# Text order for ScalarE and VectorE in a seven-part output projection, modulation rows two ahead, and a matmul of ones behind each flip

## The chip, the cores and the metric

The kernel runs on one core of one Trainium2 chip. The metric is the device time of one execution in microseconds. The kernel before takes 876.53 us (median of 3 runs, 875.68 to 877.57).

A core has five engines that run side by side: TensorE (PE: matmuls, with PEld for its weight loads), VectorE (DVE), ScalarE (ACT), GpSimd (POOL) and SyncE (SP, which here only issues DMAs). Each works through its own list of instructions in order, and semaphores hold an instruction until what it reads is there.

## The reference

The program is a backbone of two layers over 512 latent tokens and 256 context tokens, width 1024, fp32. Layer 0 mixes tokens by retention in both directions, with 4 heads; layer 1 is a chunked gMLP. Both are modulated by vectors made from a conditioning vector.

```python
for i in range(DEPTH):                                # 2 layers
    shift_x, scale_x, gate_x = jnp.split(silu_c @ ada_w[i] + ada_b[i], 3, axis=-1)
    hx = rmsnorm(x, norm_g[i]) * (1 + scale_x[:, None]) + shift_x[:, None]
    out_x, out_c = ...                                # retention (i = 0), gMLP (i = 1)
    x = x + gate_x[:, None] * out_x
return rmsnorm(x, final_g)

# retention, for each head: scores, decay mask, times v; then
o = o * lax.rsqrt(jnp.mean(o * o, axis=-1, keepdims=True) + NORM_EPS)
out = (o * jax.nn.silu(z)) @ w_out                    # w_out: 2048 x 1024
```

## The kernel before, in words

**Precision.** Every fp32 operand is held as a pair: the high part is a ScalarE cast to a short format, the low part is source minus high part, on VectorE. `split` issues these two. `mm3` makes a product of two pairs from three matmuls. So a weight tile of 128x1024 that TensorE multiplies by (named `hl`) is made from a loaded tile (`raw`) by a ScalarE cast and a VectorE subtraction.

**Seven products in place of eight.** Large products go by a scheme with seven block products (a class `Product`). The weight blocks are the quarters B11, B21, B22 as loaded, and the sums T1 and T2 (two raws added on VectorE), T3 and T4 (in this projection added by a DMA that accumulates, issued by POOL). The other operand is split into quarters too: A11, A12, A22 and the sums S1 to S4. The order of the products is B11, B21, T1, T2, B22, T3, T4, with A11, A12, S1, S2, S4, S3, A22.

**The order of instructions.** TensorE's is the order of the text. For ScalarE and VectorE a scheduler chooses, unless the text pins it: while `act.pinned` and `dve.pinned` are set, the class `Queue` ties each instruction of that engine to the one before it in the text. `aside` runs one step of a side job (a Python generator) with both pinned.

**The weight stream.** The object `Q` loads raws, adds T1 and T2, and splits into four `hl` buffers in rotation. `Q.get()` hands out the next tile and first brings the stream two tiles further (`upto`); `upto` ends by doing the raw sum of the tile after that, ahead of its turn.

**Layer 0's second half.** `attend_two` does heads 0 and 1: for each step of two key blocks `score` (matmuls of q and k, named `qk`, into one of two PSUM buffers tagged `tm`; then `pf` = scores times decay on VectorE, and its pair `ph`, `pl`) and, two steps later, `pv` (matmuls by `v`). After the last step of a half of the queries come the root mean square `ss` and `gt` (the gated output), and a flip: eight transposes of `gt` into PSUM, then `turn`, which builds operands from them. The quarters "11", "21" and "12" lie in the buffers `w3`, `dec` and `g1`. The last flip, (1, 1), gives the operands S1, S2, S4 and A22.

`out_two` is the output projection of heads 0 and 1: 14 runs of 24 matmuls (seven names, each for two column halves q0 and q1), with the last flip inside run n = 1. The finished sums go through `snap` (PSUM copied or added) into `acc` by ScalarE. Side jobs run between: `vs` (v of head 2), `ds` (the decay of head 2: loads into `w3` and `g1`, a ScalarE exponential that needs its table loaded, and `dt` on VectorE) and `qs` (q and k of head 2). Then `attend_one(2)`, `project_out(2)`, `attend_one(3)` and `project_out(3)` do heads 2 and 3 one by one.

**The modulation rows.** `background` forms vectors of layer 1 from 32 rows of 512 KB (`ada_piece`): one row is loaded into a `bg` buffer, and the step after multiplies it by a value and adds it to `ada_a` on VectorE. Its steps are spread through layer 0 by hand. Vector 3 (i = 3) uses the buffers `w2` and `w3`, with one row loaded ahead.

**Ones.** `between_modes` is one 128x128 fp32 matmul of ones by ones. It stands behind some groups of transposes or fp32 matmuls, among them the last flip of head 1.

## Time and profile before

| | before |
|---|---|
| median of 3 runs | 876.53 us (875.68 to 877.57) |
| the profiled execution | 875.56 us, span 873.8 us |
| TensorE busy | 856.6 us (98%) |
| VectorE busy | 709.4 us (81%) |
| ScalarE busy | 479.9 us (55%) |
| GpSimd busy | 84.8 us (10%) |

All times in views of the trace count from the start of the span. Nearly all engine work stands under one line, L54, the helper that records it, so the names of tiles tell what an instruction is: in `hl<-raw,hl` the low part of a weight tile is formed, in `quarter<-pst,quarter` an operand sum, in `oA<-quarter,oA` or `oS<-quarter,oS` its low part. The seven-part projection is the stretch from 380.7 to 425.8 us.

### The profile page before, as it was taken

The page shows a single profiled execution, that of the slowest core. Times are in us where ns is not written, and L with a number is a line of the kernel's source. Part 1 is how long each engine was busy: PE and PEld are TensorE (multiplying, and loading weights), DVE is VectorE, ACT ScalarE, POOL GpSimd, SP SyncE. Part 2 cuts the span into 40 slices and gives each one's busy share as a digit, 9 for nine tenths or more (in the row PEclk, how much of TensorE's full clock was granted, in tenths as well). Part 3 has the DMA queues.
Part 4 walks back from the last instruction along what each step waited for, and adds up shares of the span by engine and source line. Part 5 has one row for each costly group of instructions (what it writes and reads, how often), then busy time and mean ns, then how long its engine had stood idle before and what let it go on. Part 6 is the DMA issues. An engine that isn't in the chain of part 4 may idle for free.

```text
span 873.8 us, 17037 instructions
## 1 busy us (share of the span) xinstructions
PE 856.6 (98%) x6820; PEld 818.0 (94%) x6820; DVE 709.4 (81%) x1003; ACT 479.9 (55%) x757; POOL 84.8 (10%) x127
## 2 busy tenths in 40 slices
PE   8999999999999999999999999999999999999996
PEld 7899999999999999889989899999999899899985
DVE  4799899969968875897677879998888478678895
ACT  5466544464355346657672549744666456255434
POOL 0001211211211010010100002021000000000110
PEclk9999999999999999999999999999999999999998
DMA  9945867868967796258984642657555246146532
GB/s 360 403 122 151 248 193 270 254 201 242 303 188 223 232 337 199 87 151 272 239 288 150 217 105 109 203 148 236 175 146 191 51 146 203 39 145 194 121 48 97
DMA packets 78126, 167.96 MB, mean 192 GB/s; under 512 B 8160, under 2 KB 33248, under 8 KB 78048
## 3 DMA queue, kind: packets, MB, share of 16 engines
q1 hardware_dynamic: 65280, 126.30, 43.4%
q0 software_dynamic: 12336, 40.38, 18.3%
q8 instruction: 53, 0.87, 0.4%
q10 hardware_dynamic: 432, 0.20, 0.1%
q14 instruction: 25, 0.20, 0.1%
HBM read 128.58 MB, written 24.12 MB: 175 GB/s over the span
## 4 chain that ended last, share of the span: by engine, by line
PE 81%; DVE 8%; DMA 7%; ACT 2%; issue 1%; DVEq 0%; SPq 0%; ACTq 0%
PE pst L54 81%; DMA ada_w<-in_ada_dram 2%; DVE hl L54 2%; DMA cq<-in_cT_dram 1%; DVE v L54 1%; DMA bg<-in_adag_dram 1%; DVE gt L54 1%; DMA qk<-q 1%; DMA bg<-in_dec_dram 1%; DVE ada_a L54 1%; DMA vt<-vt 1%; DVE quarter L54 1%; DMA raw<-in_w_dram 1%; DVE pf L54 0%; DMA cv<-in_cv_dram 0%
## 5 line engine op out<-in xcount | busy, mean ns | idle before, releaser
L54 DVE TENSOR_TENSOR hl<-raw,hl 128x1024 fp32r<-128x1024 f32 (+2 forms) x203 | 242.5, 1199 | 71.8 <-ACT hl L54 71.3
L54 ACT CAST hl<-raw 128x1024 fp32r<-128x1024 f32 (+2 forms) x203 | 208.3, 1031 | 155.7 <-PE pst L54 70.6
L54 PE MATMUL pst<-oS,hl 128*128 128x256 f32 x1296 | 157.4, 280 | 2.3 <-DVE hl L54 1.8
L54 PEld LDWEIGHTS pst<-oS,hl 128*128 128x128 f32 x1296 | 152.5, 190 | 3.6 <-DVE hl L54 2.1
L54 PE MATMUL pst<-hl,oS 128*128 128x256 f32 x1152 | 134.4, 276 | 0.0
L54 PE MATMUL pst<-oA,hl 128*128 128x256 f32 x1080 | 134.3, 280 | 0.1
L54 PEld LDWEIGHTS pst<-hl,oS 128*128 128x128 f32 x1152 | 132.3, 188 | 0.8 <-ACT hl L54 0.4
L54 PEld LDWEIGHTS pst<-oA,hl 128*128 128x128 f32 x1080 | 127.8, 188 | 2.0 <-ACT oS L54 0.4
L54 PE MATMUL pst<-hl,oA 128*128 128x256 f32 x768 | 92.4, 277 | 0.0
L54 DVE TENSOR_TENSOR raw<-raw 128x1024 f32<-128x1024 f32 x73 | 88.8, 1219 | 0.8
L54 PEld LDWEIGHTS pst<-hl,oA 128*128 128x128 f32 x768 | 89.4, 188 | 0.0
L54 ACT ACTIVATE snap<-pst 128x512 f32<-128x512 f32 x81 | 48.2, 595 | 63.3 <-PE pst L54 63.2
L54 PE MATMUL pst<-v,ph 128*128 128x512 f32 x192 | 59.8, 393 | 0.0
L54 PE MATMUL pst<-hl,ya 128*128 128x512 f32 (+1 forms) x246 | 59.1, 386 | 0.0
L187 POOL DMA_DIRECT2D raw<-raw x27 | 23.5, 869 | 365.1 <-DVE raw L54 145.5
L54 DVE TENSOR_TENSOR snap<-snap,pst 128x512 f32<-128x512 f32 x75 | 51.0, 680 | 6.2 <-PE pst L54 5.9
L54 PEld LDWEIGHTS pst<-hl,ya 128*128 128x128 f32 x246 | 45.3, 188 | 9.5
L54 PE MATMUL pst<-og,hl 128*128 128x256 f32 x384 | 46.6, 280 | 0.0
L54 PEld LDWEIGHTS pst<-og,hl 128*128 128x128 f32 x384 | 45.0, 188 | 0.4 <-DVE og L54 0.3
L54 PEld LDWEIGHTS pst<-v,ph 128*128 128x128 f32 x192 | 36.1, 188 | 7.1
L54 PEld LDWEIGHTS pst<-qk 128*128 128x128 f32 x288 | 35.8, 188 | 3.9 <-DVE pf L54 2.8
L54 PE MATMUL pst<-qk 128*128 128x256 f32 x288 | 36.8, 280 | 2.6 <-DVE pf L54 2.6
(222 smaller groups left out, 1085.6 us busy)
## 6 DMA issues: line engine op xcount, KB each, us to landing
raw<-in_w_dram SPq DMA_DIRECT2D x224, 256.0 KB, 3.8
bg<-in_adag_dram SPq DMA_DIRECT2D x32, 512.0 KB, 4.9
raw<-raw POOLq DMA_DIRECT2D x27, 512.0 KB, 5.1
ada_w<-in_ada_dram SPq DMA_DIRECT2D x16, 512.0 KB, 9.1
raw<-in_w_dram SPq DMA_DIRECT2D x16, 512.0 KB, 4.4
bg<-in_dec_dram SPq DMA_DIRECT2D x12, 512.0 KB, 5.1
v<-snap POOLq DMA_DIRECT2D x16, 256.0 KB, 4.4
z<-snap POOLq DMA_DIRECT2D x16, 256.0 KB, 4.6
```

The lines of the kernel that those rows point to most:

```text
L54: made = op(*args, **kw)
L187: nc.gpsimd.dma_start(self.raws[q, to], self.raws[q, src], accum_op=ALU.add)
```

## The change

In `out_two` ScalarE and VectorE are pinned from the first run to the last, the raw sums T1 and T2 are no longer done ahead of their turn, and tiles are taken three ahead in place of two. The operand sums S1, S2, S4 and A22 are taken out of the flip into a generator, `sums`, whose steps run after the products n = 1, 3, 5 and 6. The side jobs are spread anew; the last steps of `vs` go to the first two steps of `attend_one(2)`. Vector 3 of the modulation uses three buffers and loads two rows ahead; its steps and some of the earlier ones move. A matmul of ones ends every flip (eight); the two that stood at single flips are dropped.

```diff
@@ Stream
+            self.eager = True
...
-            if self.limit is None or self.done < self.limit:
+            if self.eager and (self.limit is None or self.done < self.limit):
                 self.sum(self.done)
@@ modulation rows
-    def ada_piece(i, tag, tags):
+    def ada_piece(i, tag, tags, ahead=1):
...
-            if k < KT:
+            for j in range(len(rows), min(k + ahead, KT)):
                 rows.append(bg_raw(tags))
-                load(rows[k], adag_d[8 * i + k])
+                load(rows[j], adag_d[8 * i + j])
...
-            for a in ada_piece(i, *(("g1", row_tags) if i < 3 else ("oA22", ("w2", "w3")))):
+            for a in ada_piece(i, *(("g1", row_tags) if i < 3 else ("oA22", ("w2", "w3", "g1"), 2))):
...
+    def bound(work):
+        before = act.pinned
+        act.pinned = dve.pinned = True
+        r = work()
+        act.pinned = dve.pinned = before
+        return r
+
     def aside(work):
-        act.pinned = dve.pinned = True
-        r = next(work, None)
-        act.pinned = dve.pinned = False
-        return r
+        return bound(lambda: next(work, None))
...
-            if 2 not in pieces and i in {... 3: (0, 2, 4, 6), 5: ...}.get(n, range(7)):
+            if 2 not in pieces and i in {... 3: (0, 2, 3, 4, 5, 6), 4: (0, 2, 3, 4, 6), 5: ...}.get(n, range(7)):
                 pieces.append(step())
@@ attend
             if (h, hf) == end:
-                due.pop(0)()
+                bound(due.pop(0))
...
                 flipped.append(pq.rearrange("p (b t) -> p b t", b=2))
+            between_modes()
             turn(h, hf, flipped)
...
+        for i in range(2):
+            plan[i, 2] += [of(work) for work in own]
@@ attend_two
         def turn(h, hf, flipped):
-            act.pinned = dve.pinned = True
-            (quarter_11, quarter_21, quarter_12, quarter_22)[2 * h + hf](flipped)
-            act.pinned = dve.pinned = False
+            if (h, hf) == (1, 1):
+                last.append(flipped)
+            else:
+                bound(lambda: (quarter_11, quarter_21, quarter_12)[2 * h + hf](flipped))
...
-        def quarter_22(flipped):
+        last = []
+
+        def sums():
+            flipped = last.pop()
             for r, src in zip(parts("21"), flipped):
                 dve.tensor_tensor(r, src, r, ALU.subtract)
             halved("S1", at["21"])
+            yield
             for r, src in zip(parts("11"), flipped):
                 dve.scalar_tensor_tensor(r, src, -1.0, r, ALU.mult, ALU.subtract)
             halved("S2", at["11"])
+            yield
             for r, src in zip(parts("12"), flipped):
                 dve.tensor_tensor(r, src, r, ALU.add)
             halved("S4", at["12"])
+            yield
             halved_parts("A22", flipped)
+            yield
...
-                (11, 2): [more, ahead(1)], (12, 2): [q2, ahead(2)]}
-        return attend((0, 1), plan, turn)
+                (11, 2): [more, ahead(1)], (12, 2): [ahead(2)], (13, 2): [ahead(3)]}
+        return attend((0, 1), plan, turn), sums()
@@ out_two
-        def turned():
-            flip()
-            between_modes()
...
-        n = 0
+        n, Q.eager = 0, False
+        act.pinned = dve.pinned = True
         for name in PAIRED:
             for q in OUT0:
-                w = Q.get()
+                w = Q.get(3)
                 if n == 1:
-                    inside.append(turned)
+                    inside.append(flip)
                 prods[q].run(name, w)
                 for work in works.get(n, ()):
                     aside(work)
                 n += 1
-        Q.free[:] = []
+        act.pinned = dve.pinned = False
+        Q.free[:], Q.eager = [], True
@@ project_out
-                if then is None and hf == 1:
+                if then is None and (hf == 1 or c == 3):
                     step()
...
-                        if (hf, m, kk) == (0, 4, 1) and then is None:
-                            between_modes()
@@ heads 0 to 3
-    out_two(flip, {6: (vs, ds), 8: (vs, qs), 9: (ds,), 10: (vs, qs), 11: (vs, ds), 12: (vs, qs), 13: (vs, vs)})
+    out_two(flip, {1: (ss,), 3: (ss,), 5: (ss,), 6: (vs, ss), 7: (ds,), 8: (vs, qs), 9: (ds, qs), 10: (vs, vs, qs), 11: (ds,),
+                   12: (vs,)})
...
-    og, flip = attend_one(2, qs, vs, load_wo(2), (2, 3, 5, 6))
+    og, flip = attend_one(2, qs, vs, load_wo(2), (2, 3, 5, 6), (own,))
+    drained(own)
...
-    og, flip = attend_one(3, iter(()), iter(()), load_wo(3), (0, 1, 2, 3, 5, 6))
+    og, flip = attend_one(3, iter(()), iter(()), load_wo(3), (1, 2, 3, 5, 6))
```

The numbers behind names in the pieces below tell one tile from another; each kernel has its own.

VectorE in the first half of the seven-part projection, before: `oS1` is the low part of S2, `oS2` of S4, `hl_5000` that of T2 q1, `hl_5030` and `hl_5070` those of B22 q0 and q1.

```order
L54 TENSOR_TENSOR oS1_4872<-quarter_4507,oS1_4872 128x1024
L54 TENSOR_TENSOR quarter_4777<-pst_4855,quarter_4777 128x512
L54 TENSOR_TENSOR quarter_4777<-pst_4860,quarter_4777 128x512
L54 TENSOR_TENSOR snap_4899<-snap_4899,pst_4939 128x512
L54 TENSOR_TENSOR hl_4968<-raw_4545,hl_4968 128x1024
L54 TENSOR_TENSOR oS2_4877<-quarter_4777,oS2_4877 128x1024
L54 TENSOR_TENSOR oA22_4880<-pst_4855,oA22_4880 128x512
L54 TENSOR_TENSOR oA22_4880<-pst_4860,oA22_4880 128x512
L54 TENSOR_TENSOR raw_4547<-raw_4745,raw_4547 128x1024
L54 TENSOR_TENSOR hl_5030<-raw_4743,hl_5030 128x1024
L54 TENSOR_TENSOR hl_5070<-raw_4745,hl_5070 128x1024
L54 TENSOR_TENSOR hl_5000<-raw_4547,hl_5000 128x1024
```

The same place now: `oA11` is the low part of S1, `hl_4895` that of T1 q1, `hl_4928` that of T2 q0.

```order
L54 TENSOR_TENSOR quarter_4656<-pst_4862,quarter_4656 128x512
L54 TENSOR_TENSOR quarter_4656<-pst_4867,quarter_4656 128x512
L54 TENSOR_TENSOR oA11_4890<-quarter_4656,oA11_4890 128x1024
L54 TENSOR_TENSOR raw_4549<-raw_4745,raw_4549 128x1024
L54 TENSOR_TENSOR hl_4895<-raw_4549,hl_4895 128x1024
L54 TENSOR_TENSOR snap_4843<-snap_4843,pst_4898 128x512
L54 TENSOR_TENSOR raw_4547<-raw_4747,raw_4547 128x1024
L54 TENSOR_TENSOR hl_4928<-raw_4547,hl_4928 128x1024
L54 TENSOR_TENSOR snap_4886<-snap_4886,pst_4931 128x512
L54 SCALAR_TENSOR_TENSOR quarter_4509<-pst_4862,quarter_4509 128x512
L54 SCALAR_TENSOR_TENSOR quarter_4509<-pst_4867,quarter_4509 128x512
L54 TENSOR_TENSOR oS1_4961<-quarter_4509,oS1_4961 128x1024
```

Each raw sum and each operand sum is now followed at once by the low part of the same tile, and T2 q1's low part no longer stands behind those of B22.

ScalarE in the second half, before: `hl_5099`, `hl_5133`, `hl_5169` and `hl_5203` are the tiles of T3 q0, T3 q1, T4 q0 and T4 q1, `bg` is the decay.

```order
L54 CAST hl_5070<-raw_4745 128x1024
L54 CAST hl_5000<-raw_4547 128x1024
L54 ACTIVATE snap_5057<-pst_4811 128x512
L54 CAST hl_5099<-raw_4739 128x1024
L54 ACT_TABLE_LOAD
L54 ACTIVATE bg_5062<-bg_5062,lg_181 128x512 x2
L54 ACTIVATE snap_5097<-pst_4842 128x512
L54 CAST hl_5133<-raw_4741 128x1024
L54 CAST hl_5169<-raw_4549 128x1024
L54 ACTIVATE acc_4237<-snap_5057,gate0_895 128x256 x2
L54 CAST qk_4520<-qk_4520 128x512
L54 CAST hl_5203<-raw_4737 128x1024
```

Now, with `hl_5068`, `hl_5106`, `hl_5140` and `hl_5178` for the same four tiles:

```order
L54 CAST hl_5068<-raw_4743 128x1024
L54 ACTIVATE snap_5095<-pst_4849 128x512
L54 ACT_TABLE_LOAD
L54 ACTIVATE bg_5098<-bg_5098,lg_181 128x512 x2
L54 CAST hl_5106<-raw_4745 128x1024
L54 ACTIVATE acc_4237<-snap_5059,gate0_895 128x256 x2
L54 CAST qk_4520<-qk_4520 128x512
L54 CAST hl_5140<-raw_4551 128x1024
L54 ACTIVATE acc_4237<-snap_5095,gate0_895 128x256 x2
L54 ACTIVATE bg_5100<-bg_5100,lg_181 128x512 x2
L54 CAST qk_4522<-qk_4522 128x512
L54 CAST hl_5178<-raw_4741 128x1024
```

Before, one of the four casts stood ahead of the table load and two together right behind the decay; now T3 q1's follows the decay, and acc and qk pieces (ahead of the last also an exponential) stand ahead of each of the two of T4.

VectorE at the start of head 3, before (`bg` to `ada_a` is a modulation row, `acc` an addition of `project_out(2)`, `pf` and `pl` belong to the first score):

```order
L54 SCALAR_TENSOR_TENSOR ada_a_5396<-bg_5773,cpad_175,ada_a_5396 128x1024
L54 SCALAR_TENSOR_TENSOR acc_4237<-pst_5838,gate0_895,acc_4237 128x256
L54 SCALAR_TENSOR_TENSOR acc_4237<-pst_5852,gate0_895,acc_4237 128x256
L54 SCALAR_TENSOR_TENSOR ada_a_5396<-bg_5804,cpad_175,ada_a_5396 128x1024
L54 SCALAR_TENSOR_TENSOR pf_5881<-pst_5868,dt_5587 128x512
L54 TENSOR_TENSOR pl_5884<-pf_5881,ph_5883 128x512
L54 SCALAR_TENSOR_TENSOR ada_a_5396<-bg_5835,cpad_175,ada_a_5396 128x1024
```

And now:

```order
L54 SCALAR_TENSOR_TENSOR ada_a_5402<-bg_5755,cpad_175,ada_a_5402 128x1024
L54 SCALAR_TENSOR_TENSOR acc_4237<-pst_5818,gate0_895,acc_4237 128x256
L54 SCALAR_TENSOR_TENSOR acc_4237<-pst_5832,gate0_895,acc_4237 128x256
L54 SCALAR_TENSOR_TENSOR ada_a_5402<-bg_5786,cpad_175,ada_a_5402 128x1024
L54 SCALAR_TENSOR_TENSOR acc_4237<-pst_5847,gate0_895,acc_4237 128x256
L54 SCALAR_TENSOR_TENSOR acc_4237<-pst_5861,gate0_895,acc_4237 128x256
L54 SCALAR_TENSOR_TENSOR pf_5890<-pst_5877,dt_5597 128x512
L54 TENSOR_TENSOR pl_5893<-pf_5890,ph_5892 128x512
```

The last row of the vector, `bg_5835` before and `bg_5786` now, has moved from behind the first `pf` to two additions ahead of it.

10 lines of the change are left out of this document (5 added, 5 removed).

## The prediction

> **What bounds the kernel now.** I read the chain of waits on the page first, then a table by stretches, then the order of events around each hole in TensorE's row. The chain that ended last:
>
> ```profile
> PE 81%; DVE 8%; DMA 7%; ACT 2%; issue 1%; DVEq 0%; SPq 0%; ACTq 0%
> ```
>
> TensorE sets the time; the rest is short holes in which it waits. VectorE's 8% is the share a change of order on VectorE can touch. Next the stretches that the edits reach (from:to, length, then busy time of PE, PEld, DVE, ACT and POOL, the granted clock, DMA share, GB/s):
>
> ```profile
> 179.00:229.00 50.00, 49.97 (x441) 49.24 (x440) 42.76 (x55) 23.78 (x32) 6.59 (x11) 1.00 0.77 232
> 386.00:404.00 18.00, 16.57 (x141) 16.36 (x140) 18.00 (x21) 13.32 (x19) 1.68 (x2) 1.00 0.65 203
> 404.00:426.00 22.00, 21.58 (x170) 21.59 (x171) 12.51 (x17) 15.04 (x25) 2.53 (x3) 0.92 0.84 255
> 404.00:408.00 4.00, 3.58 (x18) 3.59 (x19) 1.50 (x2) 2.36 (x4) 0.00 (x0) 0.59 0.99 252
> 482.00:486.00 4.00, 4.00 (x25) 3.51 (x25) 3.20 (x5) 1.45 (x3) 0.00 (x0) 1.00 0.34 108
> ```
>
> The second row decides: in the first half of the seven-part projection VectorE is busy 18.00 of 18.00 us. It has no slack at all there, so whatever makes it wait lands on TensorE. In the second half it is busy 12.51 of 22. Now that place in order of time (start, duration, engine, operation; in brackets the idle time before and what ended it):
>
> ```profile
> 383.17 0.15 DVE L54 RECIPROCAL ss<-ss 128x2 f32<-128x2 f32 x1
> 383.24 1.20 DVE L54 TENSOR_TENSOR hl<-raw,hl 128x1024 fp32r<-128x1024 f32 x1
> ...
> 384.36 1.40 DVE L54 SCALAR_TENSOR_TENSOR gt<-pst,ss,z 128x512 f32<-128x512 f32 x2
> ...
> 386.64 0.39 PE L54 MATMUL pst<-ones 128*128 128x128 f32 x2
> 386.78 1.66 PE L54 MATMUL pst<-oS,hl 128*128 128x256 f32 x12
> 386.81 1.28 DVE L54 TENSOR_TENSOR quarter<-pst,quarter 128x512 f32<-128x512 f32 x2
> 388.01 1.21 DVE L54 TENSOR_TENSOR raw<-raw 128x1024 f32<-128x1024 f32 x1
> 388.12 1.05 ACT L54 CAST oA<-quarter 128x1024 fp32r<-128x1024 f32 x1 [2.93 <-DVE quarter L54]
> 388.27 11.47 PE L54 MATMUL pst<-oA,hl 128*128 128x256 f32 x96
> ...
> 389.21 1.23 DVE L54 TENSOR_TENSOR oA<-quarter,oA 128x1024 fp32r<-128x1024 f32 x1
> ...
> 391.55 0.68 DVE L54 TENSOR_TENSOR snap<-snap,pst 128x512 f32<-128x512 f32 x1
> ...
> 399.58 2.99 PE L54 MATMUL pst<-oS,hl 128*128 128x256 f32 x24
> ...
> 400.88 4.62 DVE L54 TENSOR_TENSOR hl<-raw,hl 128x1024 fp32r<-128x1024 f32 x4
> ...
> 404.42 3.91 PE L54 MATMUL pst<-oS,hl 128*128 128x256 f32 x18 [1.85 <-DVE hl L54]
> ```
>
> Three things are to be seen. A split is a chain of three: VectorE makes the source (386.81, two pieces, 1.28), ScalarE casts it (388.12, 1.05), VectorE takes the low part (389.21, 1.23), with some 0.03 between them. While ScalarE casts, VectorE does a raw sum that belongs to another tile (388.01): the free order fills the 1.1 us. And the free order has a fault: the low part for T2 q1 stands last of the four at 400.88, and TensorE waits 1.85 us for it. After that wait the clock is 0.59 for four microseconds; over the 22 us it is 0.92, so 22 x 0.08 = 1.8 us are lost on top. This one place costs 1.85 + 1.8 = 3.6.
>
> Then the end of the projection and the start of head 2:
>
> ```profile
> 400.19 0.38 SPq L54 DMA_DIRECT2D bg<-in_dec_dram  x1
> ...
> 405.76 1.28 ACT L54 ACT_TABLE_LOAD   x1 [1.63 <-DMA bg<-in_dec_dram]
> 407.06 1.34 ACT L54 ACTIVATE bg<-bg,lg 128x512 f32<-128x512 f32 x2
> ```
> ```profile
> 412.86 0.91 ACT L54 ACTIVATE acc<-snap,gate 128x256 f32<-128x256 f32 x2
> ...
> 413.67 0.60 ACT L54 CAST qk<-qk 128x512 fp32r<-128x512 f32 x1
> ...
> 423.21 0.84 ACT L54 ACTIVATE acc<-pst,gate 128x256 f32<-128x256 f32 x2
> ...
> 423.94 1.04 ACT L54 CAST v<-v 128x1024 fp32r<-128x1024 f32 x1
> ...
> 425.02 1.23 DVE L54 TENSOR_TENSOR v<-v 128x1024 fp32r<-128x1024 f32 x1 [1.05 <-ACT v L54]
> 425.84 4.40 PE L54 MATMUL pst<-qk 128*128 128x256 f32 x36
> ...
> 427.45 0.69 DVE L54 SCALAR_TENSOR_TENSOR pf<-pst,dt 128x512 f32<-128x512 f32 x1 [1.21 <-PE pst L54]
> ...
> 428.65 0.63 ACT L54 CAST ph<-pf 128x512 fp32r<-128x512 f32 x1
> 430.33 0.68 DVE L54 TENSOR_TENSOR pl<-pf,ph 128x512 fp32r<-128x512 f32 x1
> ...
> 431.06 0.50 PE L54 MATMUL pst<-v,pl 128*128 128x512 f32 x1 [0.83 <-DVE pl L54]
> ```
>
> Here TensorE waits 0.83, for a `pl` behind two `v` parts. The third hole is at the start of head 3, where a score's `pf` stands behind a modulation row that has not landed (the last row here is from the page's list of DMA issues: count, KB, median us to landing):
>
> ```profile
> 469.39 1.27 DVE L54 SCALAR_TENSOR_TENSOR ada_a<-bg,cpad,ada_a 128x1024 f32<-128x1024 f32 x1
> ...
> 470.69 7.00 SPq L54 DMA_DIRECT2D bg<-in_adag_dram  x3
> ...
> 476.03 2.88 PE L54 MATMUL pst<-qk 128*128 128x256 f32 x24
> ...
> 477.26 0.87 DVE L54 SCALAR_TENSOR_TENSOR acc<-pst,gate,acc 128x256 f32<-128x256 f32 x2
> ...
> 479.54 1.28 DVE L54 SCALAR_TENSOR_TENSOR ada_a<-bg,cpad,ada_a 128x1024 f32<-128x1024 f32 x1 [1.41 <-DMA bg<-in_adag_dram]
> ...
> 481.48 1.65 PE L54 MATMUL pst<-qk 128*128 128x256 f32 x12 [2.56 <-DVE pf L54]
> ```
> ```profile
> bg<-in_adag_dram SPq DMA_DIRECT2D x32, 512.0 KB, 4.9
> ```
>
> All that the change can win is 3.6 + 0.83 + 2.56 = 7 us.
>
> **The change part by part**, on the clock of the run before.
>
> *Text order, first half.* VectorE now has sum, low part, operand sum, low part in the order of the program, and each low part waits for a cast that cannot start before the VectorE instruction just ahead of it is done. Nothing of another tile stands between. A T tile costs 1.2 (sum) + 1.05 (cast) + 1.2 (low) = 3.45; an operand sum 1.28 + 1.05 + 1.2 = 3.5; a plain tile 1.2, since its cast has been done. `gt` no longer stands behind the low part of 383.24, so it ends at 383.3 + 1.2 = 384.5 in place of 385.76, and TensorE reaches B21 1.2 earlier, at 387.0. From 384.5: two plain low parts to 386.9; T1 q0's tile to 390.35; S1 to 393.9; T1 q1's tile to 397.3; snap 0.68 and T2 q0's tile to 401.45; snap 0.68 and S2 to 405.65. TensorE needs 11.47/96 = 0.12 us a matmul, 2.87 a run. B21 from 387.0 ends at 392.8, T1 q0 waits 1.1 for S1, T1 q1 0.5 for its tile, and T2 q0, which could start at 400.2, waits until 405.65: **5.4 us**, where it started at 399.58 before. Next T2 q1's tile 409.1, B22 q0's 410.3, S4 413.9; TensorE is through T2 at 412.0, so it waits **1.9** more. At half clock (1.8 lost) it would be through at 413.8, still within this cover, so the clock after the first wait costs nothing. B22 started at 404.42 + 2.87 + 1.8 = 409.1 before and now at 413.9: +4.8. The bounds of this term: nothing, if all casts were hidden after all (the second rival), and +6.5, if one more chain falls into the path.
>
> *Text order, second half.* ScalarE too is in text order, and with it the decay of head 2. Its load goes into `g1`, the buffer of quarter "12", which is free when S4's low part is done, 413.9 (before: issue at 400.19). From issue to the table load it took 405.76 - 400.19 = 5.6, so ScalarE, which stands at this wait, goes on at 419.5, with 1.28 + 1.34 to 422.1. Queued behind it are the cast of T3 q1's tile (423.2) and its low part: 424.4. Without a wait TensorE would have begun it at 413.9 + 3 x 2.87 = 422.5: **1.9**. Then snap 0.68, acc 0.91, cast of qk 0.60, cast of T4 q0's tile 1.05, its low part 1.2: 428.85 against 424.4 + 2.87 = 427.3, **1.55**. Then snap 0.68, acc 0.91, exp 1.34, qk 0.60, cast 1.05, low part 1.2: 434.65 against 431.7, **2.95**. The projection ends at 437.5, 11.7 later than the 425.84 of before. Behind it ScalarE has acc, qk, acc, exp, acc and the cast of v (0.7 for the snap, then 0.91 + 0.60 + 0.91 + 1.34 + 0.84 + 1.04) to 441.0, VectorE v's low part to 442.2 and `pf` to 442.9; only this frees the bank for score 2. Scores 0 and 1 end at 437.5 + 24 x 0.12 = 440.4, so TensorE waits **2.5**; score 2 and `pl` (0.63 + 0.68 after `pf`) are both done at 444.3. The run before stood at this point at 431.06: **+13.2**, in which the 1.85, the 1.8 and the 0.83 of before are already gone. Low bound: if only the first half counts, 4.8 - 0.8 = +4.0. High bound: one more landing of 5.6 in the path (head 2 has three decay loads), +18.8. I take the worked value, as every piece of it is a row.
>
> *Clock after the later waits.* 0 to 1.8 in all (one drop like that at 404). The wait of 1.85 was followed by a clock of 0.59, the wait of 2.56, which ended at 481.48, by 1.00 (the stretches from 404 and from 482); one of two, so +0.8. The Trainium skill, "TensorE: Matmul & The Clock Gate", sections "What's actually happening" and "Why this matters for your kernels", lets the clock fall only after a whole idle window (some 3.4 us) and warns of gaps above about 3 us. By that rule waits of 1.5 to 2.95 cost no clock, and the sum is 0.8 lower; the stretch from 404 speaks against it, the one from 482 for it, and I keep the row.
>
> *Modulation rows.* With three buffers, row 7's load is issued once row 4 is used. Row 3 is used at 469.39 (1.3), then come an acc piece (0.4) and row 4 (1.3): 472.4; landing after 4.9 at 477.3, used by 478.6, two acc pieces (0.4 each) to 479.4, `pf` (0.69) to 480.1, against TensorE's 481.48 before: **-1.4**. Bounds: 0 (landing as late as now) and -2.56 (all of the wait). Earlier in the layer the steps move to other runs of a stretch (from 179 to 229) in which VectorE is busy 42.76 of 50 us, so 7 us hide them; were that cover gone at one place, a row would cost its 1.28. I take 0 there, bounds 0 and +1.3.
>
> *Ones behind the flips.* Six more matmuls of ones; the one of before took 386.78 - 386.64 = 0.14. Three come before the first wait and vanish in it; three count: **+0.4**. Bounds -0.6 to +0.8, since they may also shift TensorE's pace.
>
> Sum: 13.2 + 0.8 - 1.4 + 0.4 = +13.0. The profiled execution took 875.56 (span 873.8), so 888.6; the median, 876.53, lies 1.0 above it: **889**.
>
> **Rivals.**
> *Only the first half counts.* Three tiles ahead instead of two might give ScalarE enough casts in hand to get past the decay's landing, and the queue catches up by head 2. For it: VectorE has 9.5 of 22 us free in the second half. Against it: in the order of ScalarE one tile only (T3 q0's) stands ahead of the table load. It would be 4.8 - 0.8 + 0.4 - 1.4 = +3.0, with the clock 0 to 1.8 more: 879.5, range 877 to 882.
> *The casts stay hidden, and the change is faster.* One mechanism: no VectorE time is lost to casts between 384.5 and S2. Its bare work there is 2 x 1.2 + 3 x 2.4 + 2 x 2.5 + 2 x 0.68 = 16.0, so S2 is ready at 400.5, T2 q0 waits 2.0 (TensorE is there at 398.5), T2 q1 does not wait, S4 is done 1.2 + 1.2 + 1.2 + 2.5 later, and B22 starts at 406.6 in place of 409.1: -2.5. With -0.83, -1.4 and +0.4 that is -4.3: 872, range 868 to 874.7. It decides as soon as fewer than two of the five casts before S2 show as idle time of VectorE. For it: in the row of 388.01 the same work is hidden. Against it: what hid it there was a sum of another tile ahead of its turn, which text order forbids.
> That the change doesn't do what it says is ruled out by the order of instructions; the edits are all in it.
>
> **Chances.** The chain through both halves 0.74 (889, own range 882 to 896), first half only 0.14 (879.5), casts hidden 0.12 (872). A measurement of this kernel can tell about 0.2%, 1.75 us, from no change: same is 874.8 to 878.3, which takes a third of the second case and little else. Faster 0.11, same 0.05, slower 0.84. The range 877 to 896 leaves out the third case and the ends.
>
> **What would show it.** TensorE holes ahead of T2 q0 (about 5.4), B22 q0 (1.9), T3 q1, T4 q0, T4 q1 (1.9, 1.6, 2.95) and score 2 of head 2 (2.5); VectorE no longer 18.00 of 18.00 but with idle times of 1.1 ended by ScalarE's hl, oA and oS; a table load that waits for the decay's DMA until about 419.5; at head 3 a `pf` wait of about 1.2. I am wrong on the first half if T2 q0 starts before 402, on the second if score 0 of head 2 starts less than 8 us later than before, and on the sign if the holes at T2 are shorter than 1.85 together.

## The result and the profile after

The changed kernel takes 897.03 us (median of 4 runs, 895.27 to 898.65), the kernel before in the same comparison 876.6 (875.68 to 877.57): a ratio of 1.0233, 95% interval 1.021 to 1.0255, or 20.4 us slower. The prediction was 889, range 877 to 896. The direction was right. The slowdown is 1.6 times the forecast one (12.5), and the time lies 1 us outside the range. The profiled execution took 898.65, span 896.9: it is the slowest of the four, so its trace shows 23.1 us where the medians differ by 20.4.

The chain of waits and two stretches of the profile after; the stretches are those of before from 386 and from 404, taken six later, because TensorE reaches B21 that much later:

```profile
PE 79%; DVE 9%; DMA 6%; ACT 3%; issue 2%; DVEq 0%; SPq 0%; ACTq 0%
```
```profile
392.00:410.00 18.00, 14.07 (x100) 13.89 (x99) 12.36 (x15) 7.55 (x10) 2.61 (x3) 0.81 0.63 147
410.00:432.00 22.00, 16.23 (x136) 15.44 (x135) 11.20 (x12) 11.10 (x15) 0.83 (x1) 1.00 0.73 227
```

VectorE was busy 18.00 of 18.00 us in the first half of the projection. Now it is busy 12.36, with TensorE waiting for it: its work has not grown, its idle time has. Where the time is lost, in order (timeline of the changed kernel). First, long before the projection, in the stretch where modulation steps were moved:

```profile
209.01 1.28 DVE L54 SCALAR_TENSOR_TENSOR ada_a<-bg,cpad,ada_a 128x1024 f32<-128x1024 f32 x1 [4.22 <-DMA bg<-in_adag_dram]
...
227.83 2.79 PE L54 MATMUL pst<-hl,cs 128*128 128x256 f32 x12 [3.48 <-DVE ctx L54]
```

VectorE stands 4.22 us at a row that has not landed; fifteen microseconds later its lag reaches TensorE as a hole of 3.48, with a slow clock behind it (0.91 over the 20 us from 228). B21 starts at 393.87, where it was 388.27 before: 5.6 us are gone before the projection begins. Then its first half:

```profile
393.87 5.82 PE L54 MATMUL pst<-oA,hl 128*128 128x256 f32 x48
...
399.32 1.22 DVE L54 TENSOR_TENSOR raw<-raw 128x1024 f32<-128x1024 f32 x1
...
400.57 1.04 ACT L54 CAST hl<-raw 128x1024 fp32r<-128x1024 f32 x1 [2.43 <-DVE raw L54]
401.65 1.22 DVE L54 TENSOR_TENSOR hl<-raw,hl 128x1024 fp32r<-128x1024 f32 x1 [1.11 <-ACT hl L54]
...
402.79 0.68 DVE L54 TENSOR_TENSOR snap<-snap,pst 128x512 f32<-128x512 f32 x1
...
403.62 8.19 PE L54 MATMUL pst<-oA,hl 128*128 128x256 f32 x48 [3.93 <-DVE snap L54]
...
411.64 2.88 PE L54 MATMUL pst<-oS,hl 128*128 128x256 f32 x24
```

Here is the chain of the prediction: sum, cast, low part, with VectorE idle 1.11 during the cast. But the hole is not ahead of T2 q0, where it was forecast (5.4), but ahead of T1 q0 (3.93), and it is ended by a `snap`. T1 q0 writes into the PSUM bank in which B21 q0 lies (the tag `tm` has two buffers, one for each column half), and the `snap` that reads this bank stands in text order behind the tile of T1 q1. T2 q0 then follows at once. And the second half, up to the first pv of head 2:

```profile
418.45 1.23 DVE L54 TENSOR_TENSOR oS<-quarter,oS 128x1024 fp32r<-128x1024 f32 x1 [1.11 <-ACT oS L54]
...
419.73 8.32 PE L54 MATMUL pst<-oS,hl 128*128 128x256 f32 x71 [0.88 <-DVE oS L54]
...
422.70 0.38 SPq L54 DMA_DIRECT2D bg<-in_dec_dram  x1
...
428.77 1.28 ACT L54 ACT_TABLE_LOAD   x1 [6.50 <-DMA bg<-in_dec_dram]
...
433.64 5.49 PE L54 MATMUL pst<-oS,hl 128*128 128x256 f32 x24 [5.60 <-DVE hl L54]
...
443.23 0.68 DVE L54 TENSOR_TENSOR snap<-snap,pst 128x512 f32<-128x512 f32 x1
...
443.97 8.48 PE L54 MATMUL pst<-oA,hl 128*128 128x256 f32 x48 [4.83 <-DVE snap L54]
...
452.29 4.24 PE L54 MATMUL pst<-qk 128*128 128x256 f32 x36
...
456.37 0.39 PE L54 MATMUL pst<-v,pl 128*128 128x512 f32 x1
```

S4 is done at 419.7, but the load of the decay, which needs S4's buffer, is issued only at 422.70. ScalarE stands 6.50 us at it, and T3 q1 waits 5.60. The 24 matmuls behind this hole take 5.49 us and the 48 behind the next 8.48, where 2.87 and 5.74 are the full pace. The next hole, 4.83 ahead of T4 q0, is again a bank: it waits for the `snap` of T3 q0, behind the tile of T4 q1. From B21 to the first pv it now takes 456.37 - 393.87 = 62.5 us, where it took 431.06 - 388.27 = 42.8. The prediction had 444.3 - 387.0 = 57.3.

At head 3 the change does what it was forecast to do; the hole of 2.56 is one of 0.92:

```profile
505.49 1.65 PE L54 MATMUL pst<-qk 128*128 128x256 f32 x12 [0.92 <-DVE pf L54]
```

### The profile page after: what moved, and what is told of

Read it like the earlier page. It is cut to its first block, busy times and chain, and to the rows that moved or that the text cites. A ratio compares the mean times of both kernels' runs of the same rounds, so it can differ in the third digit from the quotient of the medians.

```text
span 896.9 us, 17062 instructions
## 1 busy us (share of the span) xinstructions
PE 865.4 (96%) x6832; PEld 826.8 (92%) x6832; DVE 710.7 (79%) x1003; ACT 480.2 (54%) x757; POOL 85.1 (9%) x127
## 4 chain that ended last, share of the span: by engine, by line
PE 79%; DVE 9%; DMA 6%; ACT 3%; issue 2%; DVEq 0%; SPq 0%; ACTq 0%
PE pst L54 79%; DVE hl L54 2%; DMA ada_w<-in_ada_dram 2%; DMA bg<-in_dec_dram 1%; DMA bg<-in_adag_dram 1%; DVE ada_a L54 1%; DMA cq<-in_cT_dram 1%; ACT hl L54 1%; DVE raw L54 1%; DVE snap L54 1%; ACT junk L54 1%; DMA cv<-in_cv_dram 0%; DVE v L54 0%; ACT bg L54 0%; DVE pf L54 0%
## 5 line engine op out<-in xcount | busy, mean ns | idle before, releaser
L54 PE MATMUL pst<-oA,hl 128*128 128x256 f32 x1080 | 139.4, 287 | 8.8 <-DVE snap L54 8.8
L54 PEld LDWEIGHTS pst<-oA,hl 128*128 128x128 f32 x1080 | 132.7, 195 | 11.2 <-DVE snap L54 5.1
L54 PE MATMUL pst<-v,ph 128*128 128x512 f32 x192 | 59.9, 393 | 0.0
L54 DVE SCALAR_TENSOR_TENSOR ada_a<-bg,cpad,ada_a 128x1024 f32<-128x1024 f32 x28 | 35.8, 1278 | 4.4 <-DMA bg<-in_adag_dram 4.2
```

Of the source, the lines that this page charges most:

```text
L54: made = op(*args, **kw)
```

## The experiments

In every comparison the kernel before ran on the same chip; its medians were 874.9 to 875.9. "Slower by" is always the median against that of before from the same comparison, and the ratio has its 95% interval. Beside it stands the length of the projection, from B21's start to the first pv of head 2 in the profiled execution (42.8 before, 62.5 in the changed kernel).

### The change taken apart

Four kernels, each the kernel before with one part of the change.

**Text order of the projection alone** (the parts of the diff in the stream, in the two heads and in `out_two`; the old spread, rows and ones):

```diff
         prods = {q: Product(outward, put(q[1])) for q in OUT0}
-        n = 0
+        n, Q.eager = 0, False
+        act.pinned = dve.pinned = True
...
-                w = Q.get()
+                w = Q.get(3)
```

> The text order of the projection alone (with its own tiles ahead, operand sums and side jobs); modulation steps, rows and ones as before. In the trace of the changed kernel TensorE reaches B21 5.6 us later than before (388.27, now 393.87) and the pv of head 2 25.3 us later (431.06, now 456.37). If the projection itself makes the difference of the two, this kernel is 19.7 us slower than the kernel before, about 896. By the chain of my prediction alone it would be 13.2 slower, about 890. If the projection only suffers because it starts late against its loads, it would be less than 10 slower.

Measured: 895.76 (894.37 to 897.57), 20.2 slower, 1.0233 (1.0204 to 1.0262); projection 62.7 us. So the projection makes this loss by itself, wherever it starts. Here nothing else moves its start, so its times can be laid beside the worked ones. B21, B22 and the first pv of head 2:

```profile
386.74 5.82 PE L54 MATMUL pst<-oA,hl 128*128 128x256 f32 x48
...
412.61 8.34 PE L54 MATMUL pst<-oS,hl 128*128 128x256 f32 x71 [0.87 <-DVE oS L54]
...
449.47 0.39 PE L54 MATMUL pst<-v,pl 128*128 128x512 f32 x1
```

The prediction had 387.0, 413.9 and 444.3: the first half is 1.0 us shorter than worked out, the second 6.5 longer.

**The other spread of modulation steps alone:**

```diff
-            ... 3: (0, 2, 4, 6), 5: ...
+            ... 3: (0, 2, 3, 4, 5, 6), 4: (0, 2, 3, 4, 6), 5: ...
```

> The other spread of modulation steps over the runs n = 3 and 4 of layer 0's projections alone. The changed kernel's trace has a hole of 3.48 us at 224 (TensorE waits for VectorE's ctx) and a slower clock behind it. If the spread alone makes it, this kernel is 3.5 us slower for the hole and 1.5 to 1.8 for the clock: about 881.8. If the hole needs another part of the change, the time is that of before, 876.6.

Measured: 880.21 (877.39 to 884.22), 4.6 slower, 1.0052 (1.003 to 1.0075). Its timeline, SP's queue, VectorE and TensorE:

```profile
201.26 9.50 SPq L54 DMA_DIRECT2D bg<-in_adag_dram  x4
...
207.31 1.29 DVE L54 SCALAR_TENSOR_TENSOR ada_a<-bg,cpad,ada_a 128x1024 f32<-128x1024 f32 x1 [3.22 <-DMA bg<-in_adag_dram]
...
226.14 2.93 PE L54 MATMUL pst<-hl,cs 128*128 128x256 f32 x12 [3.09 <-DVE ctx L54]
```

The spread alone makes the hole. I had costed it at nothing, as VectorE had 7 us free in the stretch. It had them, but not in the piece where it now waits.

**Ones alone** (behind every flip; the two at single flips are dropped):

```diff
                 flipped.append(pq.rearrange("p (b t) -> p b t", b=2))
+            between_modes()
             turn(h, hf, flipped)
```

> The matmuls of ones behind all eight flips alone. Six more of 0.14 us: +0.4 to +0.8, about 877.2; a change of TensorE's pace could make it -0.6 to +1.5.

Measured: 875.49 against 875.59, 0.9998 (0.9983 to 1.0012): no difference that can be told.

**Rows two ahead alone** (with the steps that use them moved as in the change):

```diff
-            for a in ada_piece(i, *(("g1", row_tags) if i < 3 else ("oA22", ("w2", "w3")))):
+            for a in ada_piece(i, *(("g1", row_tags) if i < 3 else ("oA22", ("w2", "w3", "g1"), 2))):
```

> The third vector's rows two ahead in three buffers alone, with their steps in the output projections of heads 2 and 3. The hole ahead of head 3's third score was 2.56 us; in the changed kernel it is 0.92. So 1.4 to 1.6 us faster: about 875.1. If the hole only moves, 876.6.

Measured: 871.97 against 875.59, 3.6 faster, 0.9968 (0.9953 to 0.9983). It is faster than both kernels, and by more than the 1.4 to 1.6 expected. Its timeline gives the hole of head 3 as 0.54 us in place of 2.56, a gain of 2.0; a further 1.5 of its trace come from the clock in the projection, which is told at the end. How the 3.6 of the medians divides between the two isn't shown.

### What makes the projection's loss larger than forecast

**Tiles behind the snap.** The changed kernel, but the tile three ahead is taken after the product has issued its `snap`:

```diff
-                w = Q.get(3)
+                w = Q.get(2)
                 ...
                 prods[q].run(name, w)
+                Q.upto(Q.at + 4)
```

> The changed kernel, but each tile three ahead is taken behind the product and its snap instead of ahead of them. Theory of the banks: the holes of 3.93 us (ahead of T1 q0) and 4.83 us (ahead of T4 q0) of the changed kernel are waits for a PSUM bank whose snap addition stands in VectorE's text order behind a tile that belongs two or three runs later. Then the hole at T1 q0 goes, and because VectorE's chain to S2 is as long as before, a hole of about 4.8 appears at T2 q0: no gain there. At T4 the hole falls to 1 to 2 us, and with it 2.5 to 5 us: 892 to 894.5 where the changed kernel takes 897. Theory that TensorE waits for tiles, not banks: the hole at T1 q0 stays, and the time stays within 1 us of 897.

Measured: 894.43, 19.5 slower, 1.0225 (1.0198 to 1.0252); projection 59.9. TensorE in the first half:

```profile
397.96 2.97 PE L54 MATMUL pst<-oA,hl 128*128 128x256 f32 x24 [1.46 <-DVE snap L54]
401.94 3.09 PE L54 MATMUL pst<-oA,hl 128*128 128x256 f32 x24 [1.02 <-DVE snap L54]
407.77 0.38 PE L54 MATMUL pst<-oS,hl 128*128 128x256 f32 x1 [2.73 <-ACT oS L54]
409.03 7.62 PE L54 MATMUL pst<-oS,hl 128*128 128x256 f32 x48 [0.88 <-DVE oS L54]
```

The hole of 3.93 ahead of T1 q0 has become four, 6.1 in all, and most of it now stands ahead of T2 q0. B22 follows 26.8 us after B21 (25.9 in the changed kernel): the banks decide where TensorE waits, VectorE's chain decides how long. In the trace the projection is 2.6 shorter, all of it behind B22, but the medians (19.5 slower in place of 20.4) cannot tell that from nothing.

**The decay's buffers exchanged**, so that its first row goes into the buffer that is free after S2:

```diff
-    qs, ds, vs = load_qk(2), decay(2, ("w3", "g1")), load_v(2)
+    qs, ds, vs = load_qk(2), decay(2, ("g1", "w3")), load_v(2)
```

> The changed kernel, with the two buffers of head 2's decay exchanged: the first row now goes into the buffer of quarter 11, which is free after S2, the second into that of quarter 12, free after S4. Theory of the decay: the hole of 5.60 us ahead of T3 q1 is ScalarE standing at the decay's landing (issued at 422.70, landed at 428.77). Then that hole falls below 1 us and the half clock behind it (24 matmuls in 5.5 us instead of 2.9) goes: 5.6 to 11 us less, 886 to 891.5. If the hole at T4 takes all of it over, 897.

Measured: 889.88, 14.9 slower, 1.0169 (1.0146 to 1.0191), so 5.5 less than the changed kernel; projection 54.8. From B22 to the end of T3 TensorE has no hole any more:

```profile
418.10 12.98 PE L54 MATMUL pst<-oS,hl 128*128 128x256 f32 x95 [0.88 <-DVE oS L54]
435.85 7.22 PE L54 MATMUL pst<-oA,hl 128*128 128x256 f32 x48 [4.77 <-DVE snap L54]
```

The hole ahead of T4 q0 stays at 4.77: that one is not the decay's.

**The decay's loads from POOL's queue:**

```diff
-                load(es[j], dec_d[2 * j])
+                (spill if h == 2 else load)(es[j], dec_d[2 * j])
```

> The changed kernel, with the three loads of head 2's decay issued from POOL's queue instead of SP's. In the changed kernel the buffer of the first row is free when S4's low part ends at 419.68, but SP issues the load at 422.70, behind a load of a raw, one of k and one of v that wait for buffers of their own. Theory of the queue: the load is issued some 3 us earlier against S4, the hole of 5.60 ahead of T3 q1 shrinks to about 2.6, and 2 to 3 us are gained: 894 to 895 where the changed kernel takes 897. If the landing takes as much longer from POOL, or the buffer is what counts: 897.

Measured: 890.57, 15.4 slower, 1.0173 (1.0137 to 1.0208), so 5.0 less than the changed kernel; projection 57.1.

```profile
417.13 8.34 PE L54 MATMUL pst<-oS,hl 128*128 128x256 f32 x71 [0.87 <-DVE oS L54]
417.38 0.56 POOL L142 DMA_DIRECT2D bg<-in_dec_dram  x1 [6.54 <-DVE oS L54]
422.01 1.28 ACT L54 ACT_TABLE_LOAD   x1 [2.34 <-DMA bg<-in_dec_dram]
```

The load is issued 0.25 us after S4's low part lets TensorE go on, in place of 3.0, and it is used 4.6 us later, in place of 6.1. The 3.0 were SP's queue: in the changed kernel SP stood 7.4 us at the buffer of a raw, issued that load at 420.14, two more from 420.64 and 422.22, and only then the decay's. But the place in the queue isn't all. In the kernel with tiles behind the snap SP issues the same load 0.08 us after S4 (417.52), right behind the same three loads, and it is used only 7.7 us later:

```profile
417.60 0.38 SPq L54 DMA_DIRECT2D bg<-in_dec_dram  x1
...
425.32 1.28 ACT L54 ACT_TABLE_LOAD   x1 [5.28 <-DMA bg<-in_dec_dram]
```

There T3 q1 waits 6.93. So the later issue and the longer landing both count, and the gain of 5.0, where 2 to 3 were expected, has a part of each. With the load where the prediction had put it, right behind S4, the projection takes 57.1 us, where the prediction had 57.3. That the two meet is partly luck: T3 q1 waits 1.43 and T4 q0 7.33, where 1.9, 4.5 at T4 and 2.5 at score 2 were worked out, and the landing is 1.0 shorter than assumed.

**Ones in the holes**, twice, the second time (17, 28 and 26 matmuls ahead of T1 q0, T3 q1 and T4 q0) sized so that they end with the hole:

```diff
+                if n in WARM:
+                    pr = pt((P, P))
+                    for _ in range(WARM[n]):
+                        mm(pr, ones, ones, start=True, stop=True)
                 prods[q].run(name, w)
```

> The changed kernel with matmuls of ones in three holes of TensorE: 26 ahead of T1 q0, 36 ahead of T3 q1, 32 ahead of T4 q0, at about 0.14 us each a little shorter than the holes. Nothing waits for them. Theory of the clock: the runs behind the holes take 5.5 and 8.5 us where full clock gives 2.9 and 5.8; with TensorE kept busy they run at full clock and 2.5 to 5.3 us are gained: 892 to 894.5. If the slow clock is covered by VectorE's chain everywhere, the time stays at 897.

> The changed kernel with matmuls of ones in three holes of TensorE (17 ahead of T1 q0, 28 ahead of T3 q1, 26 ahead of T4 q0), sized by their 0.22 us in a row so that none ends after the hole: with 26, 36 and 32 the clock stayed at 1.00, but the ones ended 1.1 and 0.8 us after what TensorE had waited for. Theory of the clock: 2 to 3.5 us less than the changed kernel, 893.5 to 895. If VectorE and ScalarE set the time to head 2 whatever the clock, no change: 897.

Measured: 897.55, 22.6 slower (1.0254, 1.0231 to 1.0277), with the first sizes, some of which ended after the hole; 895.88, 20.0 slower (1.0215, 1.0183 to 1.0248), with the second. In the second kernel the clock stays at full speed through the second half:

```profile
412.00:433.00 21.00, 19.42 (x169) 19.03 (x168) 9.88 (x13) 10.41 (x16) 0.00 (x0) 1.00 0.66 209
433.00:453.00 20.00, 18.76 (x155) 18.21 (x154) 12.10 (x17) 13.29 (x23) 3.36 (x4) 1.00 0.69 159
```

In the changed kernel it was 0.66 from 433 to 453. The medians cannot tell the second kernel from the changed one: it is 20.0 slower in place of 20.4, with an interval from 16.0 to 21.7. The traces tell the two holes apart:

```profile
441.11 5.92 PE L54 MATMUL pst<-oA,hl 128*128 128x256 f32 x48 [1.24 <-DVE snap L54]
```

T4 q0 starts 24.5 us after B22, which starts at 416.65 here, and 24.2 after it in the changed kernel. So the slow clock behind T3 q1's hole costs nothing: ScalarE's and VectorE's chain to that `snap` goes on meanwhile. From T4 q0 on TensorE is itself the bound, and its 48 matmuls take 5.92 in place of 8.48; in this trace the projection takes 60.3 in place of 62.5.

### The row that came late

**The other spread, with rows that take their buffers by a count of their own:**

```diff
     def bg_raw(tags):
-        spot[0] += 1
-        return st([P, 1024], tags[spot[0] % len(tags)], name="bg")
+        k = "rows" if tags is row_tags else "other"
+        spots[k] = spots.get(k, 0) + 1
+        return st([P, 1024], tags[spots[k] % len(tags)], name="bg")
```

> The other spread of modulation steps alone, as measured before (4.6 us slower than the kernel before), but the rows take their two buffers by a count of their own, so that row 1 no longer shares a buffer with row 0. Theory: with the new spread row 1 is only loaded when row 0 is used (issue at 201.26), VectorE stands 3.22 us at its landing, in text order, and the lag ends in the 3.09 us hole of TensorE at 222. Then the hole goes and the time is that of before within 1.5 us: 875 to 877. If it is the two added steps of 1.28 us in run n = 3 that make VectorE late, the hole stays: 879.5 or more.

Measured: 877.27, 1.4 slower, 1.0021 (0.9998 to 1.0045), against 4.6 for the spread alone. VectorE and TensorE:

```profile
208.39 1.29 DVE L54 SCALAR_TENSOR_TENSOR ada_a<-bg,cpad,ada_a 128x1024 f32<-128x1024 f32 x1 [1.91 <-DMA bg<-in_adag_dram]
...
225.78 2.50 PE L54 MATMUL pst<-hl,cs 128*128 128x256 f32 x10 [2.16 <-DVE ctx L54]
```

The time came out as the theory said, but the hole did not go, so the theory isn't borne out. VectorE now stands 1.91 us at row 2 in place of 3.22 at row 1, and TensorE's hole is 2.16 in place of 3.09; the clock over the 20 us from 226 is 0.92 and 0.91. In the traces B21 starts at 388.27 before, 393.08 with the spread alone and 392.05 here, so of the 4.8 us lost up to there 1.0 comes back. The rest of what the median gained need not come from the rows: in this execution the clock stayed at 1.00 in the projection, where it was 0.92 with the spread alone. So the shared buffer is a part of it, the smaller one in these traces, and a step that comes sooner than its row can land another; how the 4.6 us of the medians divides stays open, as the two intervals touch.

### What is left when the faults are mended

**Mended:** the changed kernel with tiles behind the snap, the decay's buffers exchanged and the old spread, all three edits as above.

> The changed kernel without its three separate faults: tiles three ahead behind the snap, the decay's buffers exchanged, the old spread of modulation steps. What is left of the text order is VectorE and ScalarE waiting for each other. If the parts add up (2.6, 7.1 and 4.6 less than the changed kernel): 882.5. If the waits of VectorE for casts alone are what I worked out for the first half (4.8), with rows two ahead (3.6 less): 877.8. If text order costs nothing by itself: 872.

Measured: 885.57, 9.7 slower, 1.0101 (1.0071 to 1.0131); projection 54.7. It meets none of the three times expected. The gains of the three edits alone were 0.9, 5.5 and 4.6 by the medians, 11.0 together; 10.7 came back. TensorE, and ScalarE's table load:

```profile
414.11 8.33 PE L54 MATMUL pst<-oS,hl 128*128 128x256 f32 x71 [0.88 <-DVE oS L54]
...
416.66 1.28 ACT L54 ACT_TABLE_LOAD   x1
...
437.63 4.52 PE L54 MATMUL pst<-qk 128*128 128x256 f32 x36
```

B22 starts at 414.1 and the seventh product ends at 437.6. The prediction had 413.9 and 437.5. The second agreement is luck: here ScalarE's table load waits for nothing, while the prediction had ScalarE stand at the decay's landing until 419.5.

**Mended, raw sums written ahead:**

```diff
-        n, Q.eager = 0, False
+        n, Q.eager = 0, True
```

> The mended changed kernel (885.6), still in text order, but the raw sums T1 and T2 are written right behind the low part of the tile before, as in the kernel before. Theory of the casts: VectorE's idle times of 1.1 ahead of T1 q1's, T2 q0's and T2 q1's low parts fall away, as the cast now runs beside the operand sum or the snap; S4 is done about 3 us earlier and 2 to 3 us are gained: 882.6 to 883.6. If what counts behind S4 is the decay and the acc pieces on ScalarE alone, less than 1: 884.6 or more.

Measured: 886.84, 11.6 slower, 1.0126 (1.0091 to 1.0162); projection 55.6. The forecast gain of 2 to 3 us did not come, and the theory of where VectorE's idle time comes from falls here. The timeline around T1 q1's tile:

```profile
394.72 0.68 DVE L54 TENSOR_TENSOR snap<-snap,pst 128x512 f32<-128x512 f32 x1
395.43 0.91 ACT L54 ACTIVATE acc<-snap,gate 128x256 f32<-128x256 f32 x2 [1.89 <-DVE snap L54]
...
396.25 1.03 ACT L54 CAST hl<-raw 128x1024 fp32r<-128x1024 f32 x1
397.31 1.23 DVE L54 TENSOR_TENSOR hl<-raw,hl 128x1024 fp32r<-128x1024 f32 x1 [1.91 <-ACT hl L54]
```

The sum is long done, but the cast stands behind `acc` in ScalarE's text order, and `acc` waits for the `snap` that VectorE has just finished. Each engine waits in turn for what the other did last, even with the sum written ahead. The two intervals overlap, so the kernel isn't told from the mended one by time.

**Mended, with text order on VectorE only, on ScalarE only, and on neither:**

```diff
-        act.pinned = dve.pinned = True
+        dve.pinned = True
```

The second kernel has `act.pinned = True` there, the third no such line; in all three `bound` sets each engine's flag back by itself, so that side jobs keep the order inside their steps.

> The mended changed kernel (885.6) with only VectorE in text order through the projection; ScalarE is ordered by the scheduler again. If VectorE's text order is what costs, 884 to 886. If ScalarE's order costs (acc pieces, each waiting for a snap on VectorE, stand ahead of the next cast), 877 to 880; but the scheduler now puts the first half of the decay's exponential ahead of S4's cast, which could cost up to 2 us.

> The mended changed kernel with only ScalarE in text order; VectorE is ordered by the scheduler, which puts raw sums ahead of the low parts that wait for a cast. If ScalarE's order is what costs, 884 to 886; if VectorE's, 877 to 880.

> The mended changed kernel with neither engine in text order through the projection; operand sums still apart, tiles three ahead behind the snap, side jobs as in the change, rows two ahead. If text order is the cause of what is left (9.7 us over the kernel before, 13.3 over rows alone), this is at 871 to 873. If the operand sums apart or the side jobs' places are the cause, 880 or more.

| text order in the projection | time | slower by | ratio (95%) | projection |
|---|---|---|---|---|
| both engines | 885.57 | 9.7 | 1.0101 (1.0071 to 1.0131) | 54.7 |
| VectorE only | 881.55 | 5.6 | 1.0067 (1.0043 to 1.009) | 52.2 |
| ScalarE only | 875.87 | 0.0 | 1.0003 (0.9984 to 1.0023) | 43.1 |
| neither | 871.21 | -4.7 | 0.9952 (0.9932 to 0.9972) | 40.1 |

The first half of the projection (386 to 404) in the four kernels, in the order of the table, one fence each:

```profile
386.00:404.00 18.00, 13.06 (x109) 12.49 (x107) 12.28 (x14) 7.26 (x10) 2.60 (x3) 1.00 0.64 144
```
```profile
386.00:404.00 18.00, 13.33 (x111) 12.76 (x109) 12.76 (x14) 9.77 (x14) 2.60 (x3) 1.00 0.62 142
```
```profile
386.00:404.00 18.00, 14.52 (x118) 13.91 (x118) 13.67 (x15) 9.82 (x14) 1.68 (x2) 0.99 0.71 168
```
```profile
386.00:404.00 18.00, 18.00 (x161) 18.00 (x160) 17.79 (x21) 12.58 (x18) 1.68 (x2) 1.00 0.81 209
```

The third number after the length is VectorE's busy time: 12.28, 12.76, 13.67 and, with both engines free, 17.79 of 18, and only there is TensorE busy throughout. So what the mended kernel still loses is the text order and nothing else: the operand sums apart, the side jobs' new places and the three tiles ahead are all still in the last kernel. VectorE's order alone costs 5.6 + 4.7 = 10.3, ScalarE's alone 4.7, both 14.4. The expectations had looked for one culprit, and neither kernel met them: 881.6 lies between the two times given for it, 875.9 below both. Both orders cost, VectorE's about twice as much. No kernel was run with free order and the changed kernel's own tiles ahead of the snap and decay buffers, so what those two would cost without text order isn't shown.

### Towards a faster kernel

**Before, with rows two ahead and T2 q1's low part first.** `fence` makes every later VectorE instruction of the text wait for the last one so far:

```diff
                 w = Q.get()
+                if n == 5:
+                    dve.fence()
```

> The kernel before with the modulation rows two ahead (alone 3.6 us faster), and with one order set on VectorE: nothing that comes later in the text may pass the low part of T2 q1. The hole of 1.85 us ahead of T2 q1 then shrinks, as its low part goes ahead of two tiles of B22: 1.85 less, and no clock drop behind it: 869 to 871. If VectorE, which has no slack there, then is late with B22 instead, 872.

Measured: 870.8, 4.1 faster, 0.9948 (0.9931 to 0.9966). The hole ahead of T2 q1 is nearly as long as before, so the reason was wrong even if the time was met:

```profile
403.50 13.89 PE L54 MATMUL pst<-oS,hl 128*128 128x256 f32 x120 [1.61 <-DVE hl L54]
```

**The same with A22 formed after run n = 6** (`halved_parts("A22", ...)` out of the flip into a step of its own):

```diff
             halved("S4", at["12"])
-            halved_parts("A22", flipped)
+            last.append(flipped)
...
+        def a22():
+            halved_parts("A22", last.pop())
+            yield
```

> The kernel before with rows two ahead and the order set at T2 q1 (together 870.8), and the operand A22, which only T4 needs, formed after run n = 6 instead of inside the flip. Its two low parts (1.28 us) leave the full stretch of VectorE ahead of T2 q1, whose hole is 1.78: 1.0 to 1.3 less: 869.5. If the hole at T2 q1 is ended by its cast and not by VectorE's queue: 870.8.

Measured: 870.69, 5.2 faster, 0.9937 (0.9912 to 0.9961). In its trace TensorE has no hole at T2 q1 at all, and the projection is down to 39.3 us; but the interval cannot tell this from the 4.1 without the edit.

**The same with v's last two parts in head 2's first steps**, as in the change:

```diff
-    ... 10: (vs, qs), 11: (vs, ds), 12: (vs, qs), 13: (vs, vs)})
+    ... 10: (vs, qs), 11: (vs, ds), 12: (vs, qs)})
...
+        for i in range(2):
+            plan[i, 2] += [of(work) for work in own]
```

> The kernel before with rows two ahead, the order set at T2 q1 and A22 apart (870.7), and the last two parts of v of head 2 formed in the first two steps of head 2, as the change does, so that the first pl does not stand behind them. The hole of 1.35 ahead of the first pv goes: 0.8 to 1.3 less, 869.5. If it only moves to the next pv: 870.7.

Measured: 871.86, 3.4 faster, 0.9961 (0.9942 to 0.998): nothing gained that can be told. The hole ahead of the first pv is gone (projection 38.1), but from there to the end the trace takes 3.1 us more. Two waits of 0.9, for a later `pl` at 442.3 and for `gt` at 446.2, are a part of that; the rest isn't traced.

So the part worth keeping is the smallest one, rows two ahead; with T2 q1 and A22 put right by hand, or with the change's operand sums and side jobs in free order, about 871 is reached, 25 us less than the change as it stands. The intervals do not tell these from rows two ahead alone.

## Why the prediction was wrong in size and right in direction

Its steps in their order:

- **The bound** (TensorE sets the time, VectorE has no slack in the projection's first half): right. In the mended kernel, taking text order away from both engines brings VectorE's 12.28 back to 17.79 of 18 us and 14.4 us with it.
- **"Text order, first half"**, +4.8 at B22: near in size. With text order alone B22 starts at 412.6, +3.5, and in the mended kernel at 414.1, where 413.9 was worked out. Wrong in place: I followed tiles and operands and left out the banks, so that the holes forecast ahead of T1 q0, T1 q1 and T2 q0 (1.1, 0.5 and 5.4) are one of 3.93 ahead of T1 q0, and the 48 matmuls after it take 8.19 where 5.74 are the full pace.
- **"Text order, second half"**, +13.2 at the first pv of head 2: this term was mis-sized. With text order alone it measures 449.5 - 431.1 = +18.4 in the trace. The step that failed is the sentence that the decay's load goes out when S4's low part is done and lets ScalarE go on 5.6 later. The prediction followed the buffer and not the queue in which the load stands: SP issued it 3.0 us later, it was used 6.1 after that, and T3 q1 waited 5.60 in place of 1.9. That is 3.4 of the 6.2 by which the changed kernel's trace exceeds the worked time from B22 to the first pv (36.6 against 30.4). The remaining 2.8 stand at T4, again by a bank that the prediction left out. From the table load on, the low parts of T3 q1, T4 q0 and T4 q1 follow at the distances worked out, or up to 0.6 sooner, but T4 q0 cannot use its tile until the `snap` behind T4 q1's tile has run. The two waits forecast at T4 (1.55 and 2.95) are thus one of 4.83, both runs still lie behind it, at a slow clock, and score 2 does not wait.
- **Clock**, +0.8 for the later waits: the clock fell further than that (0.66 over 20 us). Behind T3 q1's hole it costs nothing, as another chain covers it; behind T4's hole the traces with and without ones differ by 2.2 in the projection, the medians by 0.4 with an interval of several microseconds. So the term lies between nothing and some 2 us, and no run decides it closer.
- **Modulation rows**, -1.4: the hole went from 2.56 to 0.92, -1.6 in the trace. Alone this part gains 3.6 in the medians, more than the hole.
- **The spread of the steps**, "I take 0 there, bounds 0 and +1.3": wrong, and the second step that failed. It costs 4.6 alone. The cover I named (7 us free in a stretch of 50) was there, but a step in text order that stands at a landing uses it up in one place, and the bound counted a step's own 1.28 us, not its wait.
- **Ones**, +0.4: not to be told from nothing (-0.1).

The four parts alone add up to 20.2 + 4.6 - 3.6 - 0.1 = 21.1 in the medians, 20.4 together. Forecast were 14.0 for text order with its clock, 0, -1.4 and +0.4: text order cost 6.2 more than worked out, the spread 4.6 more, and the rows gave 2.2 more back. Text order alone also loses 2.3 us in its trace behind the first pv of head 2, which the prediction did not count and no run explains. That the time lies only 1 us above the range owes something to the last; the upper end allowed one more landing, but no second, separate fault. The rival of the first half alone and that of the hidden casts are both out: the second half added to the loss, and VectorE's waits for casts were in plain view.

## What to carry to other kernels

Text order on two engines that hand work to each other turns each hand-over into a wait of both; here that cost 10.3 us for VectorE, 4.7 for ScalarE and 14.4 for both. Set an order only where the free one is seen to be wrong (here one low part), and let the scheduler fill the rest. When waits are worked out by hand, follow the PSUM banks too, not the tiles and operands alone: a bank comes free when its last reader has had its turn. A load is late by its buffer, by its queue and by its landing (4.6 to 7.7 us here for the same one): before trusting a landing, look at what stands ahead of it where it is issued. When a step that waits for a DMA is moved, what it can cost is the landing, whatever slack the engine shows over a longer stretch.

## What the runs showed of the hardware that was not expected

The same hole need not slow the clock. Ahead of T2 q1 the kernel with rows two ahead waits 1.84 us, as the kernel before waits 1.85, yet its granted clock over the 22 us from 404 is 1.00 where it was 0.92:

```profile
404.00:426.00 22.00, 22.00 (x187) 22.00 (x188) 12.83 (x17) 16.91 (x28) 3.36 (x4) 1.00 0.91 268
```
```profile
403.91 14.40 PE L54 MATMUL pst<-oS,hl 128*128 128x256 f32 x120 [1.84 <-DVE hl L54]
```

The 120 matmuls behind the wait took 15.93 in the kernel before, so that is 1.5 us between two executions with the same wait in the same place. Nor does the length of the wait decide: at this place the kernel with the spread alone waits 2.09 and its clock is 0.92 over 22 us, the one whose rows have a count of their own waits 2.28 and its clock is 1.00. The Trainium skill, "TensorE: Matmul & The Clock Gate", section "What's actually happening", has a free-running window that does not start with the program. That one wait is followed by two clocks fits with this. Its idle time of a whole window (some 3.4 us), however, is longer than the 1.85 us that were enough in the kernel before; the measurement decides.

Matmuls of ones keep the clock up like any others. In the kernel with the second set of sizes, 28 of them (56 records, two to a matmul) fill 6.41 us ahead of T3 q1 and 26 fill 5.97 ahead of T4 q0, about 0.23 each, and the granted clock stays at 1.00 from 412 to 453, where it fell to 0.66 without them:

```profile
424.83 6.41 PE L54 MATMUL pst<-ones 128*128 128x128 f32 x56
...
433.90 5.97 PE L54 MATMUL pst<-ones 128*128 128x128 f32 x52
```
